# A two-layer sequence trunk on one core: in the last down stage, operand sums keep their buffers and take B21 and B22 beside the fourth and fifth product; the last four tiles' rows of x go to raw buffers

## The chip, the cores and the metric

The kernel runs on one core of a Trainium2 chip. The metric is device time in microseconds of one execution. Three runs of the kernel before took 2243.35, 2241.7 and 2243.67 us (median 2243.35). The profile is of one further execution of 2241.47 us.

## The reference, cut to what matters

Two layers over 1024 tokens of width 1024: an attention layer and a recurrent layer, each followed by a gated feed-forward block, with a norm before and behind every sub-layer. Only the feed-forward block of the second layer matters here, and of it the last matrix:

```python
def rmsnorm(x, g):
    y = x * rsqrt(mean(x * x, axis=-1, keepdims=True) + 1e-6)
    return y * g

h = rmsnorm(x, norm_ffn_pre[layer])
f = (silu(h @ w_gate) * (h @ w_up)) @ w_down      # w_down: 2816 x 1024
x = x + rmsnorm(f, norm_ffn_post[layer])
```

All is float32.

## The kernel before, in words

**Float32 products.** A float32 operand is split into a high part, a cast (ScalarE), and the remainder (VectorE). A product is then three matmuls: high by high (L731), high by remainder (L732), remainder by high (L733). A 128 x 512 split is one cast of L726 and one subtraction of L727, and makes a tile named `o`.

**The down stage** (`down`, called once for each layer) multiplies the gated activations A (2816 x 1024 tokens, kept transposed) by B = `w_down` with one level of a fast scheme of seven block products in place of eight. A's blocks and their sums (A11, S2, S3, S1, A22, S4, A12) were written to device memory by the stage before (`gA11`, `gS2` and so on; the profile writes `gA` and `gS`). B's sums are formed here, from the blocks B11, B12 (rows `block(j, 0)`) and B21, B22 (rows `block(j, 1)`). The contraction of 1408 has NP = 11 steps j of 128. The products are, in the order of the program:

1. `p1`: A11 by B11
2. `p6`: S2 by T2 = B22 - (B12 - B11), starting at j = 4
3. `p7`: S3 by T2 - B11
4. `p5`: S1 by B12 - B11
5. `p4`: A22 by T2 - B21
6. `p3`: S4 by B22
7. the loop over `a` at the end: A12 by B21

In the first six, each j takes two split operands and makes 12 matmuls, three for each of four token tiles, which add up in four banks of PSUM. The seventh goes tile by tile: all 33 matmuls of one token tile, then the next; A12 comes in three loads for each tile (`act`, two buffers), and its splits have `wb` buffers.

**Buffers.** `ts` are eleven tiles of [128, 3, 512], one for each j, in a pool of their own (`da`) that closes after product five. Their columns 0, 1 and 2 hold B11, then T2 - B11; B12 - B11; and T2. `raw` are three buffers of 4 KB a partition: each takes A's block for one j in its first half and, where a block of B is needed, that in its second (`fetch`, or L823 and L824 in `p3`). Splits go to `w` (8 buffers), `wb` (4) and `wc` (5, for B21 of j = 6 to 10 in product seven).

**Norms.** After product five the four token tiles `m2` are done: `norm(1, a, ..)` squares each (ScalarE, L178), multiplies it by the gain (VectorE, L250), takes the root on GpSimd (L182, L183), adds it scaled to x (VectorE, L256) and stores it. The store has two halves, one issued by SP and one by ScalarE (L258). The rows of x are loaded into `nx`, two buffers, two loads for each tile (L196). The four tiles `m1` are done in product seven, each with a norm behind its last sum (L848).

**Order.** Nothing is ordered by hand here, but for `load`, which puts a load behind the last fetch in the program's order. A scheduler with a model of time places each engine's instructions. They then run in that order on each engine, each waiting for what it needs. SP issues nearly all loads, in one queue in order.

Of the kernel before, what the change touches and what calls it, by code (L numbers as in the profile page):

```python
# [15 lines left out]
P = 128  # L16
S = 1024
D = 1024
# [81 lines left out]
class Trunk:  # L100
# [610 lines left out]
    def down(self, l, gO, x_src, x_dst, make_sink):  # L711
# [34 lines left out]
        with self.pool(f"d{l}") as ap:  # L746
# [3 lines left out]
            with self.pool(f"da{l}", "right") as da:  # L750

                ts = [da.tile([P, 3, 512], F32, tag="t", bufs=NP, name=self.uid("t")) for _ in range(NP)]
                n_op = [0]

                def sp(src):
                    n_op[0] += 1
                    return split(*((ap, "wb", 4) if n_op[0] % 3 == 0 else (main, "w", 8)), src)

                def fetch(name, j, src=None):
                    r = main.tile([P, 2, 512], F32, tag="raw", bufs=3, name=self.uid("raw"))  # L760
                    self.mark = nc.sync.dma_start(r[:, 0], gO[name][j]).ins
                    if src is not None:
                        nc.sync.dma_start(r[:, 1], src)
                    return r[:, 0], r[:, 1]

                def rest(j):
                    self.load(ts[j][:, 0:2], block(j, 0).rearrange("p (a b) -> p a b", a=2))
                    tt(ts[j][:, 1], ts[j][:, 1], ts[j][:, 0], op=ALU.subtract)

                def p1(j):  # L770

                    a, b = fetch("A11", j, block(j, 0, 0, 512) if j < 4 else None)
                    if j >= 4:
                        b = ts[j][:, 0]
                        rest(j)
                    return sp(a), sp(b)

                def p6(j):
                    a, b22 = fetch("S2", j, block(j, 1, 512, 512))
                    tt(ts[j][:, 2], b22, ts[j][:, 1], op=ALU.subtract)  # L780
                    if 4 <= j < 8:
                        rest(j - 4)
                    return sp(a), sp(ts[j][:, 2])

                def p7(j):
                    t = ts[j][:, 0]
                    tt(t, ts[j][:, 2], t, op=ALU.subtract)
                    return sp(fetch("S3", j)[0]), sp(t)

                def p5(j):  # L790
                    return sp(fetch("S1", j)[0]), sp(ts[j][:, 1])

                def p4(j):
# [4 lines left out]
                for m, ps in zip(m1, product(p1)):  # L798
                    nc.scalar.copy(m[:, lo], ps)
                for m, ps in zip(m1, product(p6, 4)):  # L800
                    tt(m[:, hi], ps, m[:, lo], op=ALU.add)
                gpost = self.gain(ap, "gpost", io["norm_ffn_post"][l])
                for m, n, ps in zip(m1, m2, product(p7)):
                    tt(n[:, lo], ps, m[:, hi], op=ALU.add)
                for m, n, ps in zip(m1, m2, product(p5)):
                    tt(m[:, hi], ps, m[:, hi], op=ALU.add)
                    tt(n[:, hi], ps, n[:, lo], op=ALU.add)
                for n, ps in zip(m2, product(p4)):
                    tt(n[:, lo], n[:, lo], ps, op=ALU.subtract)
            with make_sink() as sink:  # L810
# [19 lines left out]
                for j in range(NP):  # L830
                    if j % 2 == 0:
                        r = main.tile([P, 2, 512], F32, tag="raw", bufs=3, name=self.uid("raw"))
# [296 lines left out]
```

## Time and profile before

| what | us |
|---|---|
| median of three runs | 2243.35 |
| the profiled execution, whole | 2241.47 |
| its span, first to last instruction | 2239.6 |
| the last down stage: its first matmul starts | 2005.86 |
| the last matmul starts | 2228.46 |
| TensorE busy in the span | 2194.9 (98%) |

Times in the profile are microseconds from the span's start. PE is TensorE, PEld its weight loads, DVE VectorE, ACT ScalarE, POOL GpSimd, SP the engine that issues loads; SPq and ACTq are the issues of transfers. A row of a timeline has the start, the duration, the engine, the line of the kernel, the operation, its tiles (out <- in), its shape and how many are merged, and in brackets the idle time before it and what ended that.

### The profile page before, as it was taken

The page shows a single profiled execution, that of the slowest core. Times are in us where ns is not written, and L with a number is a line of the kernel's source. Part 1 is how long each engine was busy: PE and PEld are TensorE (multiplying, and loading weights), DVE is VectorE, ACT ScalarE, POOL GpSimd, SP SyncE. Part 2 cuts the span into 40 slices and gives each one's busy share as a digit, 9 for nine tenths or more (in the row PEclk, how much of TensorE's full clock was granted, in tenths as well). Part 3 has the DMA queues.
Part 4 walks back from the last instruction along what each step waited for, and adds up shares of the span by engine and source line. Part 5 has one row for each costly group of instructions (what it writes and reads, how often), then busy time and mean ns, then how long its engine had stood idle before and what let it go on. Part 6 is the DMA issues. An engine that isn't in the chain of part 4 may idle for free. (4 is left out here: it accounts for less than half of the span.)

```text
span 2239.6 us, 30733 instructions
## 1 busy us (share of the span) xinstructions
PE 2194.9 (98%) x11198; PEld 1806.9 (81%) x11198; DVE 1539.4 (69%) x2496; ACT 1146.0 (51%) x2108; POOL 227.3 (10%) x458
## 2 busy tenths in 40 slices
PE   8999999999999999999999999999999999999997
PEld 8887888878788888888887777888788888888875
DVE  5776765464877777776767677437786777759665
ACT  4544455464765444432436576528655444425433
POOL 2111212131100000000001332202000000000011
PEclk9999999999999999999999999999999999999998
DMA  5101011125523323235558411356232323237466
GB/s 168 47 27 36 25 43 41 60 98 169 183 76 113 118 90 123 90 132 201 161 168 252 131 57 48 92 195 227 75 128 98 123 90 123 90 126 259 127 202 193
DMA packets 185978, 268.92 MB, mean 120 GB/s; under 512 B 13794, under 2 KB 115170, under 8 KB 185827
## 3 DMA queue, kind: packets, MB, share of 16 engines
q1 hardware_dynamic: 185186, 264.86, 37.5%
q10 hardware_dynamic: 640, 2.10, 0.3%
q8 instruction: 88, 1.44, 0.3%
q14 instruction: 64, 0.52, 0.1%
HBM read 201.38 MB, written 65.54 MB: 119 GB/s over the span
## 5 line engine op out<-in xcount | busy, mean ns | idle before, releaser
L646 PE MATMUL ps<-hS,q 128*128 128x512 f32 (+1 forms) x1288 | 489.7, 381 | 0.7 <-ACT hS L96 0.3
L647 PE MATMUL ps<-hS,q 128*128 128x512 f32 (+1 forms) x1288 | 489.0, 380 | 0.9 <-DVE hS L89 0.9
L648 PE MATMUL ps<-hS,q 128*128 128x512 f32 (+1 forms) x1288 | 488.4, 380 | 0.0
L617 DVE TENSOR_TENSOR q<-raw,q 128x512 fp32r<-128x512 f32 x308 | 204.5, 685 | 185.7 <-ACT q L616 185.2
L647 PEld LDWEIGHTS ps<-hS,q 128*128 128x128 f32 x1288 | 242.1, 188 | 47.5 <-DVE hS L89 1.3
L646 PEld LDWEIGHTS ps<-hS,q 128*128 128x128 f32 x1288 | 241.7, 188 | 47.8 <-ACT hS L96 0.7
L648 PEld LDWEIGHTS ps<-hS,q 128*128 128x128 f32 x1288 | 242.1, 188 | 45.8
L616 ACT CAST q<-raw 128x512 fp32r<-128x512 f32 x308 | 177.3, 616 | 154.7 <-DVE raw L625 127.6
L732 PE MATMUL ps<-o,o 128*128 128x512 f32 x616 | 241.6, 393 | 3.3 <-DVE o L727 3.2
L733 PE MATMUL ps<-o,o 128*128 128x512 f32 x616 | 238.8, 392 | 0.0
L731 PE MATMUL ps<-o,o 128*128 128x512 f32 x616 | 222.2, 395 | 10.1 <-ACT o L842 6.0
L604 ACT ACTIVATE raw<-raw,gcol 128x256 f32<-128x256 f32 x352 | 150.2, 498 | 151.8 <-DMA raw<-in_ffn_w_up_dram 73.2
L726 ACT CAST o<-raw 128x512 fp32r<-128x512 f32 x206 | 123.8, 620 | 197.7 <-PE ps L733 63.8
L727 DVE TENSOR_TENSOR o<-raw,o 128x512 fp32r<-128x512 f32 x206 | 138.0, 687 | 64.3 <-ACT o L726 63.4
L182 POOL TENSOR_SCALAR rs<-ss 128x1 f32<-128x1 f32 x60 | 33.1, 551 | 1451.5 <-ACT junk L178 1367.8
L731 PEld LDWEIGHTS ps<-o,o 128*128 128x128 f32 x616 | 116.2, 189 | 38.9 <-ACT o L842 8.5
L156 DVE TENSOR_TENSOR wlo<-raw,whi 128x1024 fp32r<-128x1024 f32 x76 | 93.1, 1225 | 71.5 <-ACT whi L155 70.1
L732 PEld LDWEIGHTS ps<-o,o 128*128 128x128 f32 x616 | 116.7, 189 | 29.5 <-DVE o L727 5.3
L733 PEld LDWEIGHTS ps<-o,o 128*128 128x128 f32 x616 | 116.6, 189 | 24.6 <-DVE o L843 0.7
L155 ACT CAST whi<-raw 128x1024 fp32r<-128x1024 f32 x76 | 79.7, 1051 | 58.7 <-PE ps L167 20.2
L401 ACT COPY pt<-tr 128x512 f32<-128x512 f32 (+1 forms) x128 | 65.5, 527 | 78.6 <-PE tr L397 78.0
L166 PE MATMUL psq<-hT,whi 128*128 128x512 f32 x256 | 101.2, 395 | 1.1 <-DVE v L296 1.1
(201 smaller groups left out, 4303.4 us busy)
## 6 DMA issues: line engine op xcount, KB each, us to landing
raw<-in_ffn_w_down_dram SPq DMA_DIRECT2D x96, 256.0 KB, 4.4
raw<-in_ffn_w_gate_dram SPq DMA_DIRECT2D x44, 512.0 KB, 4.2
raw<-in_ffn_w_up_dram SPq DMA_DIRECT2D x44, 512.0 KB, 4.2
gS<-c SPq DMA_DIRECT2D x88, 256.0 KB, 3.7
raw<-gS SPq DMA_DIRECT2D x88, 256.0 KB, 2.8
gA<-c SPq DMA_DIRECT2D x66, 256.0 KB, 3.5
raw<-in_attn_w_in_dram SPq DMA_DIRECT2D x24, 512.0 KB, 4.1
raw<-gA SPq DMA_DIRECT2D x44, 256.0 KB, 2.9
```

The costliest lines, as they stand in the source:

```text
L166: nc.tensor.matmul(ps, wh[:, kt, cols], hh[:, kt, :], start=kt == 0, stop=False)
L604: nc.scalar.activation(raw[:, i], raw[:, i], AF.Copy, scale=gain[:, 4 * k + i:4 * k + i + 1])
L616: self.last = nc.scalar.copy(t[:, 0], src).ins
L617: self.last_lo = nc.vector.tensor_tensor(t[:, 1], src, t[:, 0].bitcast(F32), op=ALU.subtract).ins
L646: nc.tensor.matmul(ps, a[:, 0, kt, :], bh, start=kt == 0, stop=False)
L647: nc.tensor.matmul(ps, a[:, 0, kt, :], bl, start=False, stop=False)
L648: self.matmul = nc.tensor.matmul(ps, a[:, 1, kt, :], bh, start=False, stop=kt == 3).ins
L726: nc.scalar.copy(t[:, 0], src)
L727: tt(t[:, 1], src, t[:, 0].bitcast(F32), op=ALU.subtract)
L731: nc.tensor.matmul(ps, a[0], b[:, 0], start=first, stop=False)
L732: nc.tensor.matmul(ps, a[0], b[:, 1], start=False, stop=False)
L733: nc.tensor.matmul(ps, a[1], b[:, 0], start=False, stop=last)
```

## The change

In the last layer alone (`keep`, true where no next stage takes the result), `ts` stays until the end of the stage. Its column 0 is last read by the third product's splits, and product four loads B21 of each j into it; column 1 is last read by the fourth product's splits, and product five loads B22 into it. `p4`, `p3` and the seventh product then read these tiles, and the loads of B21 in `p4`, of B22 in `p3` and of B21 before the seventh product go. So B21 is loaded once instead of twice. The rows of x for the last four norms (`r == 0`) are loaded into `raw` buffers instead of `nx`. The first layer's stage stays as it is.

```diff
-            with self.pool(f"da{l}", "right") as da:
+            da = right.enter_context(self.pool(f"da{l}", "right"))
...
             def p5(j):
-                return sp(fetch("S1", j)[0]), sp(ts[j][:, 1])
+                a = fetch("S1", j)[0]
+                if keep:
+                    self.load(ts[j][:, 0], block(j, 1, 0, 512))
+                return sp(a), sp(ts[j][:, 1])
 
             def p4(j):
-                a, b21 = fetch("A22", j, block(j, 1, 0, 512))
-                tt(b21, ts[j][:, 2], b21, op=ALU.subtract)
-                return sp(a), sp(b21)
+                a, t4 = fetch("A22", j, None if keep else block(j, 1, 0, 512))
+                tt(t4, ts[j][:, 2], ts[j][:, 0] if keep else t4, op=ALU.subtract)
+                if keep:
+                    self.load(ts[j][:, 1], block(j, 1, 512, 512))
+                return sp(a), sp(t4)
...
+            if not keep:
+                right.close()
...
-                    self.post_norm(ms, mg, x_src, x_dst, (r, a), gpost, sink, ap)
+                    x = main.tile([P, D], F32, tag="raw", bufs=3, name=self.uid("x")) if keep and r == 0 else None
+                    self.post_norm(ms, mg, x_src, x_dst, (r, a), gpost, sink, ap, x)
...
                 def p3(j):
                     nc.sync.dma_start(r[:, 0], gO["S4"][j])
-                    nc.sync.dma_start(r[:, 1], block(j, 1, 512, 512))
-                    return split(main, "w", 8, r[:, 0]), split(ap, "wb", 4, r[:, 1])
+                    b22 = ts[j][:, 1]
+                    if not keep:
+                        b22 = r[:, 1]
+                        nc.sync.dma_start(b22, block(j, 1, 512, 512))
+                    return split(main, "w", 8, r[:, 0]), split(ap, "wb", 4, b22)
...
                 for j in range(NP):
-                    if j % 2 == 0:
-                        r = main.tile([P, 2, 512], F32, tag="raw", bufs=3, name=self.uid("raw"))
-                    nc.sync.dma_start(r[:, j % 2], block(j, 1, 0, 512))
-                    b21.append(split(*((main, "w", 8) if j < 6 else (ap, "wc", 5)), r[:, j % 2]))
+                    if keep:
+                        src = ts[j][:, 0]
+                    else:
+                        ...
+                    b21.append(split(*((main, "w", 8) if j < 6 else (ap, "wc", 5)), src))
```

Up to the last stage's fourth product every engine's instructions stand as before. Three places behind that show what moves.

SP's queue in product six, before: S4's and B22's loads of j = 6 and 7, and between them the first tiles' stores and the third tile's row loads.

```order
L823 DMA raw3177_19508<-gS4_1_6_14806 128x512
L824 DMA raw3177_19508<-in_ffn_w_down_dram 128x512
L258 DMA out_0_dram<-x3139_19326 64x1024
L196 DMA x3147_19352<-xs2_91 64x1024
L258 DMA out_0_dram<-x3143_19339 64x1024
L196 DMA x3147_19352<-xs2_91 64x1024
L823 DMA raw3180_19529<-gS4_1_7_14807 128x512
L824 DMA raw3180_19529<-in_ffn_w_down_dram 128x512
```

And with the change, from S4 of j = 6 to the rows of the tiles `x3211` and `x3224`, which are the first two of the last four:

```order
L834 DMA raw3177_19512<-gS4_1_6_14806 128x512
L834 DMA raw3180_19532<-gS4_1_7_14807 128x512
L834 DMA raw3183_19552<-gS4_1_8_14808 128x512
L834 DMA raw3186_19572<-gS4_1_9_14809 128x512
L834 DMA raw3189_19592<-gS4_1_10_14810 128x512
L258 DMA out_0_dram<-x3139_19336 64x1024
L196 DMA x3147_19362<-xs2_91 64x1024 x2
L258 DMA out_0_dram<-x3143_19349 64x1024
L196 DMA x3211_19700<-xs2_91 64x1024 x2
L196 DMA x3224_19768<-xs2_91 64x1024
L196 DMA x3151_19375<-xs2_91 64x1024 x2
```

All of S4 now stands ahead of the first store, and B22's loads are gone.

VectorE's queue at the same place, before: from the first norm's L256 to B22's split of j = 4 (`o3173`) and on.

```order
L256 SCALAR_TENSOR_TENSOR x3139_19326<-m2938_18080,rs3141_19330,x3139_19326 128x1024
L727 TENSOR_TENSOR o3178_19511<-raw3177_19508,o3178_19511 128x512
L250 TENSOR_TENSOR m2941_18083<-m2941_18083,g3027_18602 128x1024
L256 SCALAR_TENSOR_TENSOR x3143_19339<-m2939_18081,rs3145_19343,x3143_19339 128x1024
L727 TENSOR_TENSOR o3173_19472<-raw3171_19466,o3173_19472 128x512
L727 TENSOR_TENSOR o3176_19493<-raw3174_19487,o3176_19493 128x512
L727 TENSOR_TENSOR o3179_19514<-raw3177_19508,o3179_19514 128x512
L256 SCALAR_TENSOR_TENSOR x3147_19352<-m2940_18082,rs3149_19356,x3147_19352 128x1024
L727 TENSOR_TENSOR o3181_19532<-raw3180_19529,o3181_19532 128x512
```

With the change:

```order
L727 TENSOR_TENSOR o3178_19514<-raw3177_19512,o3178_19514 128x512
L727 TENSOR_TENSOR o3181_19534<-raw3180_19532,o3181_19534 128x512
L250 TENSOR_TENSOR m2939_18081<-m2939_18081,g3027_18602 128x1024
L256 SCALAR_TENSOR_TENSOR x3139_19336<-m2938_18080,rs3141_19340,x3139_19336 128x1024
L250 TENSOR_TENSOR m2940_18082<-m2940_18082,g3027_18602 128x1024
L250 TENSOR_TENSOR m2941_18083<-m2941_18083,g3027_18602 128x1024
L256 SCALAR_TENSOR_TENSOR x3143_19349<-m2939_18081,rs3145_19353,x3143_19349 128x1024
L727 TENSOR_TENSOR o3173_19477<-t2946_18091,o3173_19477 128x512
L727 TENSOR_TENSOR o3184_19554<-raw3183_19552,o3184_19554 128x512
```

S4's split of j = 7 (`o3181`) moved ahead of the norms; B22's split of j = 4 still stands behind two L256, and reads a `ts` tile (`t2946`).

VectorE's queue in product four, with the change; `o3085` to `o3089` are the splits of j = 5 and 6, `o3198` and `o3199` the first two of product seven's five `wc` splits of B21 (j = 6 and 7), and L811 sums of product three:

```order
L811 TENSOR_TENSOR m2940_18082<-ps3030_18606,m2936_18078 128x512
L727 TENSOR_TENSOR o3198_19634<-t2948_18093,o3198_19634 128x512
L811 TENSOR_TENSOR m2941_18083<-ps3031_18607,m2937_18079 128x512
L727 TENSOR_TENSOR o3085_18955<-raw3084_18952,o3085_18955 128x512
L727 TENSOR_TENSOR o3086_18958<-t2947_18092,o3086_18958 128x512
L727 TENSOR_TENSOR o3199_19637<-t2949_18094,o3199_19637 128x512
L727 TENSOR_TENSOR o3088_18976<-raw3087_18973,o3088_18976 128x512
L727 TENSOR_TENSOR o3089_18979<-t2948_18093,o3089_18979 128x512
```

These five splits stood in product seven before.

More of the change, by code (lines that the diff above doesn't have):

```diff
@@ new lines, in down @@
+            for m, ps in zip(m1, product(p1)):
+                nc.scalar.copy(m[:, lo], ps)
+            for m, ps in zip(m1, product(p6, 4)):
+                tt(m[:, hi], ps, m[:, lo], op=ALU.add)
+            gpost = self.gain(ap, "gpost", io["norm_ffn_post"][l])
+            for m, n, ps in zip(m1, m2, product(p7)):
+                tt(n[:, lo], ps, m[:, hi], op=ALU.add)
+            for m, n, ps in zip(m1, m2, product(p5)):
+                tt(m[:, hi], ps, m[:, hi], op=ALU.add)
+                tt(n[:, hi], ps, n[:, lo], op=ALU.add)
```

85 lines of the change are left out of this document (40 added, 45 removed).

## The prediction

> **What bounds the kernel now.** I read the page, then the last down stage slice by slice, then TensorE's own rows there, then who made it wait. The page says TensorE is the bound:
>
> ```profile
> span 2239.6 us, 30733 instructions
> PE 2194.9 (98%) x11198; PEld 1806.9 (81%) x11198; DVE 1539.4 (69%) x2496; ACT 1146.0 (51%) x2108; POOL 227.3 (10%) x458
> ```
>
> An average of 98% hides where the other 2% lies. The windows (PE, PEld, DVE, ACT, POOL busy with counts, then clock, DMA share and GB/s), from the fourth product on:
>
> ```profile
> 2095.00:2125.00 30.00, 30.00 (x134) 24.82 (x134) 18.99 (x31) 12.47 (x22) 0.00 (x0) 1.00 0.46 143
> 2125.00:2155.00 30.00, 30.00 (x134) 24.86 (x133) 20.46 (x33) 10.05 (x17) 0.00 (x0) 1.00 0.74 220
> 2155.00:2185.00 30.00, 24.76 (x107) 19.52 (x106) 20.17 (x25) 11.97 (x22) 8.16 (x8) 1.00 0.66 190
> 2185.00:2215.00 30.00, 26.40 (x105) 20.80 (x104) 21.42 (x33) 15.90 (x30) 2.95 (x4) 0.89 0.78 221
> ```
>
> Products four and five (first two rows) are full; six and seven have holes. TensorE's rows there (start, duration, idle before and its releaser in brackets):
>
> ```profile
> 2005.86 0.39 PE L731 MATMUL ps<-o,o 128*128 128x512 f32 x1
> 2166.91 1.07 PE L731 MATMUL ps<-o,o 128*128 128x512 f32 x4
> 2170.45 0.50 PE L732 MATMUL ps<-o,o 128*128 128x512 f32 x1 [2.47 <-DVE o L727]
> 2170.80 0.40 PE L733 MATMUL ps<-o,o 128*128 128x512 f32 x1
> 2180.08 1.19 PE L731 MATMUL ps<-o,o 128*128 128x512 f32 x4 [2.04 <-ACT o L726]
> 2183.82 0.50 PE L731 MATMUL ps<-o,o 128*128 128x512 f32 x1 [0.73 <-ACT o L726]
> 2194.63 0.50 PE L731 MATMUL ps<-o,o 128*128 128x512 f32 x1 [0.99 <-ACT o L726]
> 2195.36 0.50 PE L732 MATMUL ps<-o,o 128*128 128x512 f32 x1 [0.22 <-DVE o L727]
> 2198.71 0.80 PE L731 MATMUL ps<-o,o 128*128 128x512 f32 x1 [2.38 <-ACT o L842]
> 2202.29 0.63 PE L732 MATMUL ps<-o,o 128*128 128x512 f32 x1
> 2202.72 0.63 PE L733 MATMUL ps<-o,o 128*128 128x512 f32 x1
> 2203.48 0.39 PE L733 MATMUL ps<-o,o 128*128 128x512 f32 x1
> 2228.46 0.39 PE L733 MATMUL ps<-o,o 128*128 128x512 f32 x1
> ```
>
> A product is 11 x 4 x 3 = 132 matmuls. The first row is the stage's first matmul; the second is the first of j = 4 in product six, 5 x 132 + 48 = 708 later. So the undisturbed pitch is (2166.91 - 2005.86) / 708 = 0.2275 us. The 215 after it would start their last at 2166.91 + 215 x 0.2275 = 2215.8; it starts at 2228.46. **12.6 us are lost in the last two products**: 8.83 in the six waits, some 2.0 in the slow stretch from 2198.71 to 2203.48 (12 starts in 4.77 us instead of 2.73), the rest in the restarts.
>
> A second loss sits behind the last matmul. VectorE there:
>
> ```profile
> 2229.07 1.28 DVE L256 SCALAR_TENSOR_TENSOR x<-mg,rs,x 128x1024 f32<-128x1024 f32 x1 [1.23 <-DMA x<-xs]
> 2230.39 0.69 DVE L250 TENSOR_TENSOR mg<-m,g 128x512 f32<-128x512 f32 x1
> 2230.99 0.68 DVE L848 TENSOR_TENSOR m<-ps,m 128x512 f32<-128x512 f32 x1
> ```
>
> The last sum (L848) could start when the last matmul ends, 2228.46 + 0.39 = 2228.85. It starts **2.1 us** later, since L256 of the tile before waits for its rows of x, and those waited for a buffer of `nx`. From L848 to the end are 2239.6 - 2230.99 = 8.6 us.
>
> **Product four and five, what is added.** Product four gets eleven 256 KB loads of B21, and the five splits of B21 that have `wc` buffers move into it: 5 x 0.69 on VectorE (below) and about as much on ScalarE, against 19 and 12.5 busy in 30. DMA rises from 143 by 11 x 0.262 MB / 30 us = 96 to about 240 GB/s, a little over the 220 of the next row, where TensorE is full. Product five trades B21 for B22, one for one. I cost both at nothing. The cover is the lead of the splits:
>
> ```profile
> 2108.54 0.69 DVE L727 TENSOR_TENSOR o<-t,o 128x512 fp32r<-128x512 f32 x1
> raw<-gA SPq DMA_DIRECT2D x7, 256.0 KB, 2.7
> raw<-in_ffn_w_down_dram SPq DMA_DIRECT2D x7, 256.0 KB, 3.0
> ```
>
> The first is product four's last split; TensorE comes to it at 2005.86 + 516 x 0.2275 = 2123.2, a lead of 14.7 us. The other two are the landing times (last number) in 2095:2125. A moved split waits for its load and stands before later splits: split, issue, landing of 3.0 and two splits make some 5.3 us for two steps of j, which TensorE takes 5.4 for. So the lead stays. SP issues one load more for each j, about 0.5 us of the 2.7 that a j takes. Were the lead used up, three such chains follow one another, and each microsecond of landing over 3.0 would cost three.
>
> **Product six.** Its eleven B22 loads and product seven's eleven B21 loads go from a time when landings were long (DMA issues of 2140:2160, then of 2172:2202):
>
> ```profile
> raw<-gS SPq DMA_DIRECT2D x7, 256.0 KB, 4.7
> ...
> raw<-gS SPq DMA_DIRECT2D x4, 256.0 KB, 5.8
> x<-xs SPq DMA_DIRECT2D x7, 256.0 KB, 6.4
> out_dram<-x ACTq DMA_DIRECT2D x2, 256.0 KB, 5.1
> ```
>
> *The wait of 2.47.* VectorE is an in-order queue, and before the split that TensorE waits for it has the four sums of product five and the first norms:
>
> ```profile
> 2155.69 2.02 DVE L727 TENSOR_TENSOR o<-raw,o 128x512 fp32r<-128x512 f32 x3 [2.41 <-ACT o L726]
> 2157.63 0.68 DVE L809 TENSOR_TENSOR m<-m,ps 128x512 f32<-128x512 f32 x1
> 2168.52 1.27 DVE L256 SCALAR_TENSOR_TENSOR x<-m,rs,x 128x1024 f32<-128x1024 f32 x1
> 2169.72 1.88 DVE L727 TENSOR_TENSOR o<-raw,o 128x512 fp32r<-128x512 f32 x3
> ```
>
> From the first sum to the end of the split are 2157.63 to 2170.40, 12.8 us. The first sum is ready when product five's first tile is, 9 matmuls before 2005.86 + 660 x 0.2275 = 2156.0, so at about 2154.3; it started 3.3 us late, behind splits that waited for the S4 loads (2.41). Now S4 alone is loaded there, and j = 3 is also split by then. One more split stands in the chain: 12.8 + 0.6 = 13.4 us. TensorE needs it 52 matmuls into the product, at 2167.8. A start at 2154.7, my estimate, gives 2168.1, a wait of 0.3. Bounds: nothing, and 2.5 if the chain starts as late as it did less the 0.9 of j = 3.
>
> *The waits of 2.04 and 0.73.* SP's queue, and ScalarE at its end:
>
> ```profile
> 2171.25 0.55 SPq L258 DMA_DIRECT2D out_dram<-x  x1
> 2172.57 0.75 SPq L823 DMA_DIRECT2D raw<-gS  x1
> 2177.87 0.62 ACT L726 CAST o<-raw 128x512 fp32r<-128x512 f32 x1 [9.70 <-DMA raw<-gS]
> ```
>
> S4 of j = 7 stood behind stores that wait for VectorE's norms. All of S4 now stands before the first store, and B22 is in SBUF. What can be late next is VectorE's own queue: the norms (L256) of the third and fourth tile wait for rows of x whose `nx` buffers come free with the stores of the first two, and stand before B22's splits of j = 8 and j = 10. The second tile's L256 ended 12.2 us after the first sum, so now at about 2166.9; store 5.1, two issues 1.2 and landing 6.4 give 2179.6 at loaded times; L256 and two splits make 2182.3, and TensorE needs j = 10 at 2156.0 + 120 x 0.2275 = 2183.3. Nothing lost, with 1.0 to spare.
>
> **Product seven.** The waits of 0.99 and 0.22 are for splits of B21 that was being loaded; five are now made in product four, six from `ts`. The 2.38 is for a tile of A12 whose load landed in the loaded stretch. The same load in the loaded (2172:2202) and the quiet stretch (2205:2215):
>
> ```profile
> act<-gA SPq DMA_DIRECT2D x2, 256.0 KB, 6.5
> act<-gA SPq DMA_DIRECT2D x3, 256.0 KB, 3.0
> ```
>
> Twelve tiles go through two buffers; a round is issue 0.4, landing, cast 0.6, split 0.7, handing over 0.2. At 3.0 that is 4.9 us for two tiles, and TensorE takes 7.5 us for three: it keeps up. The third tile's buffer comes free with the first one's split, which stands three splits behind product six's last, 2182.3 + 3 x 0.7 = 2184.4. The eleventh tile's cast can start an issue, a landing and 4 rounds later, 2184.4 + 3.4 + 19.6 = 2207.4, and is needed at 2215.8 - 21 x 0.2275 = 2211.0. I take 0.2 for what I don't see.
>
> The slow stretch follows the 2.38, not the 2.47: starts 0.43 apart (2202.29, 2202.72) against 2170.80 at once. With no such wait left I take its 2.0 as gained. The Trainium skill (TensorE: Matmul & The Clock Gate, Part 1: The HAM clock gate) says that the clock is halved after about one free-running window of 3.4 us without work, and given back after a busy one. By that rule a lone wait of 2.5 costs no clock; the trace agrees, since three waits, 3.6 us in all, fell within 4.6 us before the slow stretch. By it, rival two below would stay without a slow stretch.
>
> **The tail.** Rows of x for the last four tiles are in raw buffers, three of them free after S4's last splits; their loads stand in SP's queue before the third tile's store, and the last tile's comes with the first one's store, some 8 us ahead of its use. 2.1 gained.
>
> **Sum.** 2215.8 + 0.39 + 8.6 = 2224.8 for the end of the span; with 0.5 of waits left 2225.3. The profiled execution is 2241.47, 1.87 over its span: 2227.2. It lies 1.9 under the median of the runs shown, at their lower end; half of that brings the forecast to 2228.2, that is 0.993 of before.
>
> **Rivals.**
> 1. *A12's tiles become the bound of product seven.* For it: only two buffers, and stores and row loads are still about. Against it: the quiet 3.0. At landings of 5.0, about halfway, a round is 6.9, the eleventh cast at 2184.4 + 5.4 + 27.6 = 2217.4, 6.4 late: 2235. At 6.5 it is 14 late and nearly the whole gain is gone.
> 2. *VectorE's queue stays the bound of product six.* The 2.5 above, and 1 to 2 at j = 8 and 10: 2231 to 2233.
> 3. *The chain of stores and row loads decides, and it gets slower.* A12's third tile, too, stands in SP's queue behind the fourth tile's store, so behind L256, the row load and the second tile's store. Store and landing together decide from 5.1 + 6.4 + 1.0 = 12.5 us on, one for one; for slower than before they must take some 27. Against it: fewer loads compete. From 2242 up.
> 4. *It doesn't do what it says*, so no change: the order shows the loads gone from products six and seven, which leaves little of it.
>
> **Chances.** Forecast 0.72; rival one 0.12; two 0.10; three 0.03; four 0.03. Range 2224.8 (no wait left, 2224.8 + 1.87 = 2226.7, less the 2 us by which the runs shown differ) to 2234.5 (through rival two, into rival one). Faster by over 0.2%, about what a measurement here can tell, is below 2238.9: 0.94, with 0.03 for each of the others.
>
> **What would show it.** Right: products six and seven about 30 us each, no TensorE wait over 1 us after 2166, granted clock 1.00 throughout, last sum within 0.5 us of the last matmul, product four still 30.00 of 30. Wrong: a wait on A12's cast (rival one), on VectorE's split of j = 4, 8 or 10 (two), L256 waiting for x over 6 us (three), or a hole in product four.

## The result, and the profile after

The changed kernel took 2224.96 us, the median of four runs (2221.8 to 2227.09), against 2242.52 us for the kernel before; the ratio is 0.9927, with a 95% interval of 0.9914 to 0.994. The profiled execution took 2226.18 us, 15.3 less than that of before.

The page of the changed kernel, and its windows of 30 us from the fourth product on (columns as before):

```profile
span 2224.4 us, 30685 instructions
PE 2191.2 (99%) x11198; PEld 1807.4 (81%) x11198; DVE 1537.5 (69%) x2496; ACT 1146.0 (52%) x2108; POOL 226.8 (10%) x458
...
2095.00:2125.00 30.00, 30.00 (x134) 24.82 (x134) 23.95 (x39) 15.17 (x27) 0.00 (x0) 1.00 0.60 191
2125.00:2155.00 30.00, 30.00 (x134) 24.86 (x133) 20.89 (x35) 12.66 (x23) 0.00 (x0) 1.00 0.65 185
2155.00:2185.00 30.00, 30.00 (x134) 24.86 (x133) 24.29 (x33) 15.50 (x28) 10.63 (x8) 1.00 0.73 201
2185.00:2215.00 30.00, 30.00 (x134) 24.82 (x134) 18.64 (x27) 10.53 (x24) 6.47 (x10) 1.00 0.48 126
```

Products six and seven are as full as four and five, at full clock, and the view of TensorE's waits has no row for this stage. Product four moves 191 GB/s in place of 143, and nothing there is late.

The first and the last matmul of the stage:

```profile
2005.97 0.39 PE L731 MATMUL ps<-o,o 128*128 128x512 f32 x1
2215.19 0.39 PE L733 MATMUL ps<-o,o 128*128 128x512 f32 x1
```

They are 209.22 us apart, in the kernel before 2228.46 - 2005.86 = 222.60: 13.4 gained there. The rest of the 15.3 is in the tail, from the start of the last matmul to the end of the span: 2224.4 - 2215.19 = 9.21, before 11.14. VectorE's rows there are read below, with the experiment that explains them.

### The profile page after: what moved, and what is told of

It is laid out like the page before. It is cut to its first block, busy times and chain, and to the rows that moved or that the text cites. A ratio compares the mean times of both kernels' runs of the same rounds, so it can differ in the third digit from the quotient of the medians.

```text
span 2224.4 us, 30685 instructions
## 1 busy us (share of the span) xinstructions
PE 2191.2 (99%) x11198; PEld 1807.4 (81%) x11198; DVE 1537.5 (69%) x2496; ACT 1146.0 (52%) x2108; POOL 226.8 (10%) x458
## 5 line engine op out<-in xcount | busy, mean ns | idle before, releaser
L726 ACT CAST o<-raw 128x512 fp32r<-128x512 f32 x184 | 110.6, 620 | 161.1 <-PE ps L733 51.1
L727 DVE TENSOR_TENSOR o<-raw,o 128x512 fp32r<-128x512 f32 x184 | 123.1, 686 | 55.6 <-ACT o L726 54.9
```

Source lines behind the costliest of these rows:

```text
L726: nc.scalar.copy(t[:, 0], src)
L727: tt(t[:, 1], src, t[:, 0].bitcast(F32), op=ALU.subtract)
```

## The experiments

**How they are read.** Each kernel has a ratio to the kernel before, run on the same chip beside it. Beside that stands the length of the last down stage, from its first matmul to the end of the span, in the one profiled execution. Some kernels also wait up to 0.5 us in product one, which the change does not touch; the table leaves that out. The length is needed because executions enter this stage at different times, 2003.8 to 2012.9 us after the start, though only the kernels with a third A12 buffer and the last one in the table change anything ahead of it. L866 and L867 are the line of L848, L860 and L861 those of A12's cast and split (before L842 and L843), some moved by the line that an edit adds.

| kernel | length | first to last matmul | TensorE waits, products six and seven | tail | ratio (interval) |
|---|---|---|---|---|---|
| before | 233.74 | 222.60 | 8.83 | 11.14 | 1 |
| changed | 218.43 | 209.22 | 0 | 9.21 | 0.9927 (0.9914 to 0.994) |
| changed, again | 219.17 | 209.95 | 0.2 | 9.22 | 0.9926 (0.9909 to 0.9942) |
| rows alone | 230.22 | 218.65 | 5.95 | 11.57 | 0.9981 (0.9969 to 0.9992) |
| operands alone | 221.39 | 211.22 | 0.63 | 10.17 | 0.9954 (0.9938 to 0.9969) |
| B21 and rows | 223.94 | 214.74 | 3.95 | 9.20 | 0.9952 (0.9933 to 0.997) |
| B22 and rows | 226.94 | 216.98 | 4.9 | 9.96 | 0.9955 (0.9939 to 0.9971) |
| unread loads put back | 227.86 | 217.53 | 5.2 | 10.33 | 0.9972 (0.9962 to 0.9981) |
| before, norms put behind | 234.61 | 225.56 | 8.7 | 9.05 | 1.0001 (0.9991 to 1.0011) |
| before, third A12 buffer | 231.55 | 222.48 | 10.0 | 9.07 | 1.0009 (1.0 to 1.0019) |
| unread loads, third A12 buffer | 222.07 | 212.64 | 2.7 | 9.43 | 0.9963 (0.995 to 0.9977) |
| changed, third A12 buffer | 219.58 | 210.41 | 0.8 | 9.17 | 0.9957 (0.9943 to 0.9972) |
| unread load in product four | 218.61 | 209.53 | 0 | 9.08 | one run, 2227.09 us |
| rows in both layers | 220.30 | 210.19 | 0 | 10.11 | 0.9948 (0.9928 to 0.9968) |

None of these kernels leaves out any of the computation.

**The changed kernel again.**

> The changed kernel once more, beside the next three: the four earlier runs showed that the profiled executions enter the last down stage 2004 to 2011 us after the start, whatever was changed behind it, so each run is also read by that stage's own length, from its first matmul to the end of the span (before 233.7, changed 218.4). Expected: a length of 218.4 again (218 to 220), no TensorE wait over 1 us in the stage, and a ratio of times that covers 0.993. If the length came out at 221 or more, the 15.3 us between the two profiles would be partly one execution's luck.

Measured: 2224.87 against 2241.17 us. The length is 219.17, the only wait 0.2. So the gain is no accident of one execution, and lengths of one kernel can differ by 0.7 at least.

### The change in parts

Four kernels do only some of the change. `keep` is split into `k21` (B21 is kept), `k22` (B22 is kept) and `kx` (rows in raw buffers), and each kernel sets the three:

```diff
             def p5(j):
                 a = fetch("S1", j)[0]
-                if keep:
+                if k21:
                     self.load(ts[j][:, 0], block(j, 1, 0, 512))
...
-                a, t4 = fetch("A22", j, None if keep else block(j, 1, 0, 512))
+                a, t4 = fetch("A22", j, None if k21 else block(j, 1, 0, 512))
...
-                if keep:
+                if k22:
                     self.load(ts[j][:, 1], block(j, 1, 512, 512))
...
-                    x = main.tile([P, D], F32, tag="raw", bufs=3, name=self.uid("x")) if keep and r == 0 else None
+                    x = main.tile([P, D], F32, tag="raw", bufs=3, name=self.uid("x")) if kx and r == 0 else None
...
-                    if not keep:
+                    if not k22:
                         b22 = r[:, 1]
...
-                    if keep:
+                    if k21:
                         src = ts[j][:, 0]
```

**Rows alone** (the last four tiles' rows in raw buffers; B22 and B21 loaded as before):

```diff
+        k21, k22, kx = keep and False, keep and False, keep and True
```

> Only the last part of the change: the last four tiles' rows of x go to raw buffers, and B22 and B21 are loaded in products six and seven as before. My theory: the waits of products six and seven come from those loads and the queues around them, so they stay (TensorE idle some 9 us after 2166), and only the 2.1 us come back by which the last sum stood behind a norm that waited for rows. Time before less 2: about 2240.5 (2239 to 2242). Rival: the four row loads, waiting for buffers in the transfer queue, were what held the loads behind them in product seven; then the 2.38 and the slow stretch go too, and the time is about 2236.

Measured: 2240.69 against 2245.79 us, a gain of 0.0019 of that, 4 us; the length is 3.5 shorter. TensorE's rows with a wait in products six and seven, and then VectorE's rows at the end:

```profile
2174.27 0.50 PE L732 MATMUL ps<-o,o 128*128 128x512 f32 x1 [2.30 <-DVE o L727]
2183.31 1.21 PE L731 MATMUL ps<-o,o 128*128 128x512 f32 x4 [1.49 <-ACT o L726]
2187.31 1.20 PE L731 MATMUL ps<-o,o 128*128 128x512 f32 x4 [0.95 <-ACT o L726]
2199.58 0.50 PE L731 MATMUL ps<-o,o 128*128 128x512 f32 x1 [0.75 <-ACT o L861]
2201.46 0.50 PE L732 MATMUL ps<-o,o 128*128 128x512 f32 x1 [0.46 <-DVE o L727]
```

```profile
2226.32 0.56 DVE L862 TENSOR_TENSOR o<-act,o 128x384 fp32r<-128x384 f32 x1 [1.72 <-ACT o L861]
...
2229.44 1.28 DVE L256 SCALAR_TENSOR_TENSOR x<-mg,rs,x 128x1024 f32<-128x1024 f32 x1 [1.23 <-POOL rs L183]
...
2231.37 0.68 DVE L867 TENSOR_TENSOR m<-ps,m 128x512 f32<-128x512 f32 x1
```

Product six keeps its three waits. In product seven the 2.38 and the slow stretch are gone, as the rival said, though the 7 us that it gave the kernel were too much. And the tail, which I expected back, is still 11.57 long. Its L256 waits 1.23, now for GpSimd's `rs`, where in the kernel before the same 1.23 stood to the rows of x. But there, too, the rows were in time. They were issued from 2219.59 on and took 3.8 us to land, some 5 us before their L256 started at 2229.07; what ended just ahead of it was `rs`, at 2228.47 + 0.57 = 2229.04:

```profile
2219.59 1.09 SPq L196 DMA_DIRECT2D x<-xs  x2
...
2228.47 0.57 POOL L183 TENSOR_TENSOR rs<-rs,neghalf 128x1 f32<-128x1 f32 x1
```

So rows that come in time do not shorten the tail. What the two kernels share is the chain on VectorE: A12's last split, the third tile's sum, that tile's norm with its 1.23, the last sum. In the kernel before:

```profile
2225.95 0.56 DVE L843 TENSOR_TENSOR o<-act,o 128x384 fp32r<-128x384 f32 x1 [3.60 <-ACT o L842]
2226.43 0.68 DVE L848 TENSOR_TENSOR m<-ps,m 128x512 f32<-128x512 f32 x1
```

From the last split to the last sum that is 2230.99 - 2225.95 = 5.04 us, and 2231.37 - 2226.32 = 5.05 here; with operands alone, with B22 and rows, and with the unread loads it is 5.04 or 5.05 too. In the changed kernel the split starts 5.65 us ahead of the last matmul (2.51 in the kernel before), and the sum waits for TensorE instead:

```profile
2209.54 0.56 DVE L861 TENSOR_TENSOR o<-act,o 128x384 fp32r<-128x384 f32 x1 [0.44 <-ACT o L860]
...
2215.61 0.69 DVE L866 TENSOR_TENSOR m<-ps,m 128x512 f32<-128x512 f32 x1 [0.94 <-PE ps L733]
```

The spare is 0.94. **The tail is the end of A12's chain**, not of the rows'.

**Operands alone** (the last rows of x in `nx`, as before):

```diff
+        k21, k22, kx = keep and True, keep and True, keep and False
```

> Only the first part of the change: B21 and B22 come into the operand sums' buffers beside products four and five, the rows of x stay in their own two buffers. My theory: no TensorE wait over 1 us in products six and seven, as in the changed kernel, and a last sum that starts some 2 us after the last matmul: changed kernel plus 2, about 2227 (2226 to 2228). Rival: the rows were only late because the transfers were crowded; without the 22 loads they are in time in their own buffers too, the last sum follows the last matmul within 0.5 us, and the time is the changed kernel's, 2225.

Measured: 2236.14 against 2245.79 us; the length is 221.39, 2.2 to 3.0 over the changed kernel's two. Two waits of 0.3 are left, on A12's cast and split, and the last sum is 0.9 late, behind A12's last split. SP's queue ahead of A12's third tile, here and then in the changed kernel:

```profile
2183.86 0.44 SPq L196 DMA_DIRECT2D x<-xs  x1
2184.40 1.14 SPq L258 DMA_DIRECT2D out_dram<-x  x1
2185.58 4.45 SPq L196 DMA_DIRECT2D x<-xs  x3
2190.08 14.51 SPq L196 DMA_DIRECT2D act<-gA  x7
```

```profile
2175.69 1.23 SPq L196 DMA_DIRECT2D x<-xs  x2
2179.92 0.49 SPq L258 DMA_DIRECT2D out_dram<-x  x1
2182.92 13.05 SPq L196 DMA_DIRECT2D act<-gA  x7
```

Row loads that wait for an `nx` buffer hold A12's tiles behind them: 2190.08 is 178.7 us after the stage's first matmul (2011.41), 2182.92 is 177.0. The split that frees the third tile's buffer had ended 2.7 us before that load with operands alone, and just before it in the changed kernel. So the raw buffers for the rows pay in product seven, by letting the queue past, and only through it in the tail. Neither my theory nor the rival had this: mine had the tail back by another way, the rival had no loss at all.

**B21 and rows** (B22 loaded in product six as before), **and B22 and rows** (B21 loaded twice as before):

```diff
+        k21, k22, kx = keep and True, keep and False, keep and True
```

```diff
+        k21, k22, kx = keep and False, keep and True, keep and True
```

> B21 alone is kept (loaded once in product four, its splits from the sums' buffers); B22 is loaded in product six as before. My theory: product six keeps its own three waits (2.47, 2.04 and 0.73 before; 4 to 6 us in all), since the store ahead of the S4 and B22 loads is still there, and product seven loses its 0.99, 0.22, 2.38 and the slow stretch: about 2230.5 (2229 to 2232). Rival, that only the sum of bytes in the two products counts: half of them are gone, and half of the 12.6 us comes back in both products: waits of 2 to 3 us in product six and about 2 in product seven, 2231, the same time with another split. A second rival: with B22's loads left to stand alone nothing is late any more, 2226.

> B22 alone is kept (loaded in product five); B21 is loaded twice, the second time in front of product seven, as before. My theory: product six loses its three waits (5.2 us), since S4 alone is loaded there and stands before the first store; product seven's B21 loads start earlier but still share the queue with two stores, row loads and A12's tiles: one or two waits on B21 splits or A12's casts, 1 to 4 us in all: about 2228 (2226 to 2230). Rival one, each product's waits are its own loads' alone: all 3.6 us and the slow stretch of 2.0 stay, 2231. Rival two, product seven was late only because product six's loads had run late: nothing is left, 2225.

Measured: 2235.4 and 2235.59 against 2245.79 us, 10 less, where I had 13 and 15 less; the lengths are 223.94 and 226.94, 9.8 and 6.8 less. The view of TensorE's waits with B21 and rows (total, times, longest), and two of TensorE's four rows with a wait in products six and seven with B22 and rows:

```profile
PE ps L731 <- ACT o L726: 4.0, 4, 1.6
```

```profile
2168.47 0.50 PE L732 MATMUL ps<-o,o 128*128 128x512 f32 x1 [2.34 <-DVE o L727]
...
2212.67 0.50 PE L731 MATMUL ps<-o,o 128*128 128x512 f32 x1 [1.95 <-ACT o L861]
```

With B21 kept, product seven has no wait, and product six has 4.0 us, as much as I gave it (4 to 6), but in four waits and without the 2.47: they are all ScalarE's casts in j = 7 to 10, whose S4 and B22 load behind the stores. With B22 kept these are gone, and the 2.47 of VectorE's chain stays (2.34), where I had it going. Product seven waits for A12. So the two halves cure different waits than the prediction said: the 2.04 and 0.73 come with B22's loads, while the 2.47 goes with the start of VectorE's chain. Its first sum, counted from the stage's first matmul, and the wait on the split of j = 4:

| kernel | first sum after | wait, j = 4 |
|---|---|---|
| changed | 148.0 | 0 |
| operands alone | 148.1 | 0 |
| unread load in product four | 148.1 | 0 |
| B21 and rows | 148.7 | 0 |
| changed, again | 149.0 | 0.2 |
| rows in both layers | 149.2 | 0 |
| changed, third A12 buffer | 149.4 | 0.8 |
| unread loads put back | 150.6 | 1.3 |
| before, third A12 buffer | 151.6 | 2.7 |
| rows alone | 151.7 | 2.3 |
| before | 151.8 | 2.5 |
| B22 and rows | 152.0 | 2.3 |
| unread loads, third A12 buffer | 152.2 | 2.7 |

TensorE comes to that split 161.4 to 162.3 us after its first matmul, and the wait follows the start of the chain, counted from there, almost one for one. (With rows in both layers TensorE comes late, at 162.2, and so does not wait.) So the chain is the cause. What sets its start is which splits of S4, and at times B22, stand ahead of it and when their loads land; that differs from kernel to kernel, and I can't give it to one load.

### Bytes or order

**Unread loads put back.** The 22 removed loads are put back into SP's queue, into raw buffers that nobody reads:

```diff
                     nc.sync.dma_start(r[:, 0], gO["S4"][j])
                     b22 = ts[j][:, 1]
+                    if keep:
+                        nc.sync.dma_start(r[:, 1], block(j, 1, 512, 512))
...
                         src = ts[j][:, 0]
+                        if j % 2 == 0:
+                            r = main.tile([P, 2, 512], F32, tag="raw", bufs=3, name=self.uid("raw"))
+                        nc.sync.dma_start(r[:, j % 2], block(j, 1, 0, 512))
```

> The changed kernel, with the 22 loads that it removed put back at their old places in the transfer queue, into raw buffers that nobody reads: the same bytes and the same queue as before, but no split waits for them (B22 and B21 are read from the sums' buffers). Rows of x stay in raw. My theory, that the waits were for the landing of those loads and for what they held up at a buffer: S4's loads and A12's tiles now only feel the traffic (landings of 4 to 6 us again in place of 2.6 to 3.1) and the loads' places in the queue: 1 to 5 us lost, last stage 219.5 to 223.5 long, about 221.5, time about 2228. Rival, that crowded transfers as such cost the 12.6 us: S4 and A12's tiles are as late as before, 8 to 12 us lost in products six and seven, stage 226 to 231, time 2234 to 2237.

Measured: 2234.79 against the changed kernel's 2224.87 us; the length is 227.86. 8.7 to 9.4 us of the 15 are lost again though nothing waits for these loads, within the 8 to 12 of the rival and not the 1 to 5 of my theory. Two of its waits; the cast of A12's tenth tile; and A12's loads of 256 KB issued in 2182:2202 (the last number is the landing time), here and then in the changed kernel:

```profile
2167.49 0.50 PE L732 MATMUL ps<-o,o 128*128 128x512 f32 x1 [1.32 <-DVE o L727]
...
2213.07 0.50 PE L731 MATMUL ps<-o,o 128*128 128x512 f32 x1 [2.14 <-ACT o L865]
```

```profile
2212.40 0.62 ACT L865 CAST o<-act 128x512 fp32r<-128x512 f32 x1 [5.60 <-DMA act<-gA]
```

```profile
act<-gA SPq DMA_DIRECT2D x4, 256.0 KB, 4.0
```

```profile
act<-gA SPq DMA_DIRECT2D x6, 256.0 KB, 3.0
```

Most of the loss is A12's: 3.9 of the 5.2 us of waits, and the tail. So **product seven's loss needs no dependence on B21; the loads ahead of A12's in the queue, and the slower landings, do it**. Product six loses 1.3 in place of 5.2, but there the old queue did not come back: the last of B22's loads is issued ahead of the first store,

```profile
2161.23 0.43 SPq L837 DMA_DIRECT2D raw<-in_ffn_w_down_dram  x1
2162.85 0.51 SPq L258 DMA_DIRECT2D out_dram<-x  x1
```

where in the kernel before S4 and B22 of the last four steps stood behind it. So this kernel does not show whether the 2.04 and 0.73 came from waiting for B22 or from that place in the queue.

**The kernel before, norms put behind.** All loads as before; the four norms, row loads and stores that follow product five stand behind product six's last split and load on their engines:

```diff
-            nc.scalar.copy(t[:, 0], src)
-            tt(t[:, 1], src, t[:, 0].bitcast(F32), op=ALU.subtract)
+            self.made = [nc.scalar.copy(t[:, 0], src).ins,
+                         tt(t[:, 1], src, t[:, 0].bitcast(F32), op=ALU.subtract).ins]
...
-                for a in range(4):
+                late = make_sink is nullcontext
+                held = []
+                for a in range(0 if late else 4):
                     norm(1, a, m2[a])
...
-                    nc.sync.dma_start(r[:, 1], block(j, 1, 512, 512))
-                    return split(main, "w", 8, r[:, 0]), split(ap, "wb", 4, r[:, 1])
+                    held[:] = [nc.sync.dma_start(r[:, 1], block(j, 1, 512, 512)).ins]
+                    o = split(main, "w", 8, r[:, 0]), split(ap, "wb", 4, r[:, 1])
+                    held.extend(self.made)
+                    return o
...
                     tt(m[:, hi], ps, m[:, hi], op=ALU.add)
+                with self.behind(held):
+                    for a in range(4 if late else 0):
+                        norm(1, a, m2[a])
```

> The kernel before with all its loads, but the norms, row loads and stores of the four tiles that product five finishes stand behind product six's last split and last load. The same bytes, in another order. My theory, that the order in VectorE's queue and in the transfer queue makes product six's waits: the 2.47, 2.04 and 0.73 go (under 1 us left in product six), and product seven gets the norms and stores on top of its own loads: its waits grow from 3.6 us by some 2 to 6; last stage 230 to 236 long, about 233, time about 2240. Rival, that the loads' bytes make the waits: product six keeps 3 to 5 us of waits on splits of S4 or B22, stage 235 to 240, time 2243 to 2248.

Measured: 2241.31 against 2241.17 us; the length is 234.61. Its windows of products six and seven:

```profile
2155.00:2185.00 30.00, 30.00 (x133) 24.53 (x131) 14.89 (x21) 13.59 (x25) 3.75 (x4) 1.00 0.64 189
2185.00:2215.00 30.00, 21.26 (x70) 15.51 (x70) 22.48 (x33) 11.12 (x24) 6.22 (x8) 0.80 0.88 228
```

With all of B22's bytes, product six is full once norms, row loads and stores are out of its way. There my theory holds: loads and norms together make the waits, not the bytes. The price is paid in product seven; the stage is 0.9 longer than before. (Its first sum stood at 148.4, so it can't tell the order on VectorE from the earlier landings.)

### A12's buffers

The runs so far pointed to A12's chain through two `act` buffers. Three kernels give it a third, in both layers:

```diff
-                        r = ap.tile([P, 4, P], F32, tag="act", bufs=2, name=self.uid("act"))[:, :n]
+                        r = ap.tile([P, 4, P], F32, tag="act", bufs=3, name=self.uid("act"))[:, :n]
```

> The kernel with the 22 unread loads put back, which lost some 9 us of the 15 again, with three buffers in place of two for A12's tiles. My theory now: those loads cost time only through A12's chain (3.9 of its 5.7 us of waits, and the tail) and 1.8 on splits in product six; the third buffer takes the first away: last stage 227.9 down to 220.5 to 223, about 221.5, time about 2229. Rival: crowded transfers make every landing late, more buffers or not: stage 226 to 228, time 2233 to 2235.

Measured: 2232.89 against 2241.47 us; the length is 222.07 in place of 227.86, as expected, and one wait is left, that on the split of j = 4:

```profile
PE ps L732 <- DVE o L727: 2.7, 1, 2.7
```

All waits on A12 are gone at the same traffic, so it was the round of two buffers that turned slow landings into waits. The whole time does not show the gain (2232.89 where I had 2229, and an interval that overlaps that of the unread loads with two buffers): this execution enters the stage at 2009.0, that one at 2003.8.

> The kernel before with one edit: three buffers in place of two for A12's tiles in the down stages (in both layers). All loads and norms stay where they were. The runs so far point to A12's chain (issue behind the loads and stores in the transfer queue, landing, cast, split, then the buffer's next round) as what is late in product seven and, through the last split, in the tail: in seven kernels the last sum comes 4.6 us after the third tile's, which stands right behind A12's last split. My theory now: with a third buffer the twelve tiles need a round less; the 2.38, the slow stretch of 2.0 and the tail's 2.1 go, while product six's 5.2 and the 1.2 on B21's splits stay: last stage 226 to 229 long in place of 233.7, about 227.5, time some 6 less than before. Rival: the splits of B21, or the crowded transfers, hold product seven whatever A12 has: stage 231 to 234, time less 0 to 2. The prediction's own reading of the tail (L256 waits for rows of x) would leave the tail's 2.1 in place.

Measured: 2243.65 against 2241.47 us; the length is 231.55, 2.2 less than before in place of 6. The rival was right. The waits by releaser, and the end on VectorE:

```profile
PE ps L731 <- ACT o L726: 4.6, 4, 3.3
PE ps L732 <- DVE o L727: 4.1, 3, 2.7
PE ps L731 <- ACT o L842: 1.2, 1, 1.2
```

```profile
2226.51 1.28 DVE L256 SCALAR_TENSOR_TENSOR x<-mg,rs,x 128x1024 f32<-128x1024 f32 x1 [3.12 <-DMA x<-xs]
...
2229.46 0.69 DVE L848 TENSOR_TENSOR m<-ps,m 128x512 f32<-128x512 f32 x1 [0.93 <-PE ps L733]
```

Product seven's waits add up to 3.6 us, as before, but now 2.3 of them are for splits of B21 that is still being loaded: two late things lay over one another, and taking one away uncovers the other. (Product six waits 6.4 in place of 5.2; there is no slow stretch.) The tail is the 2.1 shorter, and this with rows of x that are now truly late (L256 waits 3.12) and cost nothing: the last sum waits for TensorE. That settles the tail.

> The changed kernel with three buffers in place of two for A12's tiles. It has no wait left in the last stage, and its last sum waits for TensorE with 0.4 to 0.9 us to spare. My theory: the spare grows, the last stage stays at 218.4 to 219.2, and only the first layer's product seven, which waits 3.5 us for A12's casts, can gain: 0 to 4 us less than the changed kernel, about 2223. Rival: the third tile buffer lets A12's loads into the queue earlier, against S4's; a wait of 1 to 2 us in product six, 2226 to 2227.

Measured: 2231.72 us, ratio 0.9957, slower than the changed kernel's 0.9926; the length is 219.58, one wait of 0.8. The last stage gains nothing, having no wait for A12 to lose. The first layer, which the edit also touches, waits elsewhere:

```profile
PE pst L222 <- DVE hT L58: 3.1, 3, 2.0
PE ps L733 <- DVE o L861: 2.4, 1, 2.4
```

These are two of its rows of 1000:1300; the changed kernel has 0.2 and 0.5 there. The wait on A12's casts, which I expected to shrink, does (3.5 to 1.6), but all of the rows add up to 9.3 in place of 5.3.

### What is left

**An unread load in product four.** A second load of B21 for each j, into the free half of S1's raw buffer:

```diff
-                a = fetch("S1", j)[0]
+                a, x5 = fetch("S1", j)
                 if keep:
                     self.load(ts[j][:, 0], block(j, 1, 0, 512))
+                    nc.sync.dma_start(x5, block(j, 1, 0, 512))
```

> The changed kernel with a second load of B21, 256 KB for each j, put into product four, which nobody reads: the transfers of 2095 to 2125 rise by about 96 GB/s over the changed kernel's 191. My theory: the cover of 14.7 us in the splits' lead is far from used up: TensorE is busy 30.00 of 30 in 2095:2125, the last stage is 218.4 to 219.5 long. Rival, that the added loads are already near what the stretch can take: landings rise past 4.5 us, product four gets waits of 1 to 6 us, stage 220 to 225.

Measured: 2227.09 us in one run, length 218.61, no wait in the stage:

```profile
2065.00:2095.00 30.00, 30.00 (x134) 24.82 (x133) 16.62 (x27) 13.15 (x24) 0.00 (x0) 1.00 0.68 210
2095.00:2125.00 30.00, 30.00 (x134) 24.86 (x133) 24.10 (x39) 15.21 (x28) 0.00 (x0) 1.00 0.72 234
```

As far as one run shows, the cover of product four bears twice the load that the change put on it.

**Rows of x in raw buffers in both layers**, to beat the changed kernel:

```diff
-                    x = main.tile([P, D], F32, tag="raw", bufs=3, name=self.uid("x")) if keep and r == 0 else None
+                    x = main.tile([P, D], F32, tag="raw", bufs=3, name=self.uid("x")) if r == 0 else None
```

> The changed kernel, with the rows of x of the last four tiles in raw buffers in the first layer's down stage as well, where B21 and B22 are still loaded beside products six and seven. My theory: the first layer's product seven waits 3.5 us for A12's casts, which stand behind row loads in the transfer queue as they did in the kernel with its rows left in their own buffers: 0 to 2 us less than the changed kernel of the same chip, last stage unchanged at 218.4. Rival: raw buffers taken for rows hold up the loads that share them there, and it gets 1 to 3 us slower.

Measured: 2227.87 us, 0.9948 (0.9928 to 0.9968) beside 0.9926 (0.9909 to 0.9942) on the same chip: no gain, and the intervals overlap, so that a loss isn't shown either. The length is 220.30 and not the 218.4 that I expected; the last sum is 0.9 late behind A12's last split. In 1000:1300 the first layer's wait on A12's casts shrinks from 3.5 to 2.0, and the next stage waits instead:

```profile
PE ps L166 <- ACT hT L57: 4.3, 1, 4.3
PE ps L731 <- ACT o L860: 2.0, 2, 1.3
```

No kernel tried beats the changed one.

## Why the prediction was right

The time and the account of products six and seven were right in the main; the account of the tail was wrong, and its 2.1 us came back by another way, which was luck.

**The 12.6 us of the last two products** came back in full: 13.4 between first and last matmul in the first profile, 12.65 in the second. The undisturbed pitch is 209.22 / 923 = 0.2267 where I had 0.2275, which accounts for 0.7.

**Products four and five at nothing**: right. Neither the added load nor twice that load uses the lead up. I had all of the added 2.9 MB in 2095:2125, 240 GB/s; it spreads over two windows (107 to 165 and 143 to 191).

**The 2.47.** The chain is the cause, and the estimated start of its first sum, 2154.7, was 2153.99; the chain took 13.0 where I had 13.4, and the wait of 0.3 was 0, in the second profile 0.2. (The upper bound should read 2.3: 2157.63 - 0.9 + 13.4 is 2170.1, against 2167.8.) My reason for the early start, that S4 alone is loaded there, does not carry it: with B22 and rows S4 is alone, and the wait is 2.34.

**The 2.04 and 0.73** are loads of S4 and B22 behind stores and row loads, as I had it: shown from both sides, by B22 and rows (B22's loads gone, all of S4 ahead of the stores), and by the norms put behind (stores and rows gone). Whether S4 or B22 was the later of the two isn't told apart. Next in line I had B22's splits of j = 8 and 10 behind L256, with 1.0 to spare; no wait came.

**Product seven.** I gave 0.99 and 0.22 to B21's splits, 2.38 to A12, and expected each to go with its own loads. In fact either is late enough alone: A12 without B21's splits (unread loads put back), B21's splits without A12 (third buffer in the kernel before). The dates of A12 held: third tile free at 2184.4, issued at 2182.92; eleventh cast at 2207.4, measured 2205.77, against a need of some 2210.5.

**The slow stretch** began during the 2.38 and does not follow it, as I had read. That wait ran from 2196.33 to 2198.71, and the clock was halved before it ended (TensorE's busy time and count, clock, DMA share, GB/s):

```profile
2197.00:2198.00 1.00, 0.00 (x0) 0.50 0.97 224
```

The three waits of product seven lie within 5.1 us (2193.64 to 2198.71), not 4.6. That the 2.0 comes back when the waits go was right all the same.

**The tail**: the size was right (2.1; 1.93 measured), the cause was wrong. "L256 of the tile before waits for its rows of x" took a load that the profile names as the releaser of a 1.23 us wait for the cause of the delay. Those rows had been there for some 5 us. Other kernels have the same 1.23 on GpSimd, and one has 3.12 on the rows with no delay. It was A12's last split, 5.04 us ahead of the last sum on an in-order queue. So the step that costed the rows' raw buffers failed too: they pay 2 to 3.5 us, but in SP's queue and A12's chain.

**Sum and time.** 2224.8 for the end of the span with no wait left; it was 2224.4. The forecast of 2228.2 is 3.2 over the median: 1.0 on the profile's scale (the 0.5 of waits that did not come, and 0.4 of the span), 1.0 that I added for the median, and 1.2 by which the median here lies below the profiled execution, where in the kernel before it lay above.

**The rivals.** One (A12's tiles) is not what happened, but it is the nearest: the unread loads bring it on, and cost 9 us. Two (VectorE's queue) is what a start 2 us later would have made, as the table of first sums shows. The chain of stores and row loads decided nothing in the changed kernel; with the rows in `nx` it held A12 up by 1.7 us.

## What to carry to other kernels

The releaser that a profile names for a short wait is not always what the instruction waited for: look up when its own inputs were there, ask whether the wait would have been as long without the one named, and follow the in-order queue back from the late instruction until something is late against its own need. Two late inputs of one product cover one another: taking away one alone can return little, and a cause that both share returns all. Judge a change to one stage by that stage's own length as well as by the whole time, and count what a load does to the queue behind it, even where nobody waits for its data.

## What the runs showed of the hardware that was not expected

**The clock.** In the kernel before with a third A12 buffer a wait of 3.3 us and, later, five small ones of 3.6 us in all between 2195.9 and 2202.2 leave the clock whole. Its window of 2195:2200 (TensorE's busy time and count, clock, DMA share, GB/s), and that of the kernel before:

```profile
2195.00:2200.00 5.00, 2.90 (x9) 1.00 1.08 259
```

```profile
2195.00:2200.00 5.00, 2.39 (x7) 0.65 1.09 257
```

In the latter the clock was halved by 2197, when the waits so far were 0.99, 0.22 and the first 0.7 us of the 2.38.

In the kernel before with its norms put behind, the matmuls turn slow (0.63 in place of 0.39) without any long pause:

```profile
2190.55 0.50 PE L733 MATMUL ps<-o,o 128*128 128x512 f32 x1 [1.12 <-DVE o L850]
...
2193.48 0.79 PE L732 MATMUL ps<-o,o 128*128 128x512 f32 x1 [1.50 <-DVE o L727]
2194.07 0.63 PE L733 MATMUL ps<-o,o 128*128 128x512 f32 x1
```

No wait in that stage had been longer than 1.50 by then. The Trainium skill (TensorE: Matmul & The Clock Gate, Part 1: The HAM clock gate) gives the halved clock after at least one idle window of about 3.4 us. The trace differs, where I had written that it agrees: no stretch of that length was idle here. Small waits close together were enough in two kernels and not in a third, and one profile of each does not draw the border.

**Entering times.** In the changed kernel and in the one with operands alone every engine's instructions stand in the same order up to the last stage, and yet the latter enters it 5.4 us later. Nearly all of that is there at the transposes ahead of the second layer's feed-forward block, at 1582.87 in the changed kernel and at 1587.77 with operands alone.

The two ran on different chips, and the kernel before was 3 us slower on the second one as well (2245.79 against 2242.52 us). Beyond that the cause stays open. Such differences are why the ratios and the lengths in the table rank some kernels differently.
